# The first norm: block 0 of the context's norm ahead of the latents' statistics, modulation columns of blocks 4 to 7 loaded in pairs, matmuls at fixed places

## The chip, the cores and the metric

The kernel runs on one core of one Trainium2 chip, as one program. The metric is the device time of one execution in microseconds (us). Its engines are called by short names: PE is the matrix engine (PEld its weight loads), DVE the vector engine, ACT the scalar engine, POOL the GpSimd engine, and SP the engine that issues nearly all DMAs. Each engine takes its instructions strictly in the order in which the program lists them, and waits on semaphores for the others.

## The reference, cut to what matters

A backbone of two layers works on 256 latent tokens (x) and 256 context tokens (ctx) of width 1024. Only the head of the first layer is touched here: both streams are normed and modulated by columns that come from their conditions (c and c_ctx), and the result goes through the input projection.

```python
def rms_norm(x, g):
    xf = x.astype(F32)
    y = xf * lax.rsqrt(jnp.mean(xf * xf, axis=-1, keepdims=True) + EPS)
    return (y * g.astype(F32)).astype(x.dtype)

def adaln_norm(x, g, shift, scale):
    return rms_norm(x, g) * (1 + scale) + shift

mx = [m[:, None, :] for m in modulation(c, w_mod[l], b_mod[l])]   # silu(c) @ w + b, split in 6
mc = modulation(c_ctx, w_mod[l], b_mod[l])
h = adaln_norm(x, norm1_g[l], mx[0], mx[1])
hc = adaln_norm(xc, norm1_g[l], mc[0], mc[1])
... (hc @ w_in[l]) and (h @ w_in[l]), split into keys, values, queries, gates and so on
```

## The kernel before

Everything is kept transposed: the width of 1024 lies in 8 blocks of 128 partitions, the tokens lie along the free dimension. For accuracy each matmul operand is split into a high half (rounded) and a low half (what rounding took), and a product is three matmuls: high x high, high x low, low x high. PE is the engine that has nearly all the work.

first_norm() is the start of the program. It loads the tokens of both streams, forms their statistics (squares on ACT with a sum, then a reciprocal root by a dozen operations on 128x2 numbers on DVE, tile ss), and transposes the tokens on PE (xm). Stream 0 is the context, stream 1 the latents. Then it goes through the 8 blocks d of the width. For each block it
- multiplies the conditions by the block's modulation columns on PE ("rows", tile tp, line 592; the weights come by load_mod),
- copies the rows out (tile g) and turns them into columns by two small matmuls with the selector sel ("columns", line 607),
- forms modT (shift and scale), then na (scale times norm gain) on DVE,
- norms the block for each stream (norm_block): t = x * na * 1/rms on DVE, the high half h on ACT, and the low half h on DVE; for blocks 1, 3 and 5 (POOL_D) ACT adds the shift to t first and POOL forms the low half,
- multiplies the block's h with three chunks of the input projection (products, line 582), which accumulate over the blocks in six PSUM banks. One chunk and one block are 12 matmuls, 4 token tiles of 3.

The weights of the three chunks come in halves of four blocks (load_part): the load goes to raw or wq, ACT forms the high half (wh, br), and the low half (wl, br) is formed by POOL for chunks 0 and 2 and by DVE for chunk 1.

All DMAs of this stage are issued by SP in the order of the code, at most eight under way at a time. The order on the compute engines is set by a scheduler at build time, which follows the code and its own estimate of when operands are ready; tc.issue_after keeps an instruction behind another one. Behind the first norm the first gates follow (gates, line 345), whose weights load_w brings.

Of the kernel before, what the change touches and what calls it, by code (L numbers as in the profile page):

```python
# [10 lines left out]
F32 = mybir.dt.float32  # L11
# [5 lines left out]
ALU = mybir.AluOpType  # L17
AX = mybir.AxisListType

P = 128  # L20
D = 1024
T = 256
# [24 lines left out]
def kernel(ctx: ExitStack, tc: tile.TileContext, io, dbg=None, stop=None):  # L47
    nc = tc.nc
# [11 lines left out]
    def sb(tag, shape, dtype=F32):  # L60
        uid[0] += 1
        return pool.tile(shape, dtype, tag=tag, name=f"{tag}{uid[0]}", bufs=BUFS[tag])
# [87 lines left out]
    tp = ps("tp")  # L150
    nc.tensor.transpose(tp[:, 0:128], pk1, ident)
    nc.vector.tensor_copy(out=pkT[:, 0:128], in_=tp[:, 0:128])
    tp = ps("tp")
# [146 lines left out]
    COND = (1, 0)  # L300
# [205 lines left out]
    def first_norm():  # L506
# [6 lines left out]
        wmod, wt = {}, {}  # L513
        tags = ["r"] * 4 + ["wk"] * 2 + ["wa"] * 2 + ["a"] * 4 + ["z"] * 4

        def load_mod(d):
            wmod[d] = []
            for q in range(2):
                t_ = sb(tags[2 * d + q], [P, 4, 2, P])
                for m in range(2):  # L520
                    last_load[:] = [nc.sync.dma_start(out=t_[:, :, m, :], in_=src[:, 4 * q:4 * q + 4, m * D + d * P:m * D + (d + 1) * P])]
                wmod[d].append(t_)

        wide = []

# [11 lines left out]
            wt[ch, q] = (hi, lo)  # L537

        load_mod(0)
        load_tokens(1)  # L540
        sel = const.tile([P, 2], F32, name="sel")
        nc.vector.reduce_sum(out=sel, in_=_view(ident, 0, [(1, 2), (32, 4)]), axis=AX.X)
        rb = {}
        tps = ["mm"] * 3 + ["lv"] * 2 + ["mm"] * 3
        for st in range(2):
            ss = const.tile([P, 3, 2], F32, name=f"ss0{st}")
            for i in range(2):
                junk = sb("g2", [P, D], BF16)
                with tc.issue_after(sig.ins):
                    act(junk, tok_in[st, i], AF.Square, accum_out=ss[:, 0, i:i + 1])  # L550
            affine(ss[:, 0, :], ss[:, 0, :], 1.0 / D, EPS)
            rsqrt(ss[:, 1, :], ss[:, 0, :], ss[:, 2, :])
            for dd in range(4):
                tp = ps(tps.pop(0), (P, 2, T))
                for e in range(2):
                    for i in range(2):
                        c = (dd * 2 + e) * P
                        nc.tensor.transpose(tp[:, e, i * P:(i + 1) * P], tok_in[st, i][:, c:c + P], ident)
                if dd == 3 and st == 1:
                    nc.vector.tensor_copy(out=xT[st][:, 2 * dd:2 * dd + 2, :], in_=tp)  # L560
                else:
                    act(xT[st][:, 2 * dd:2 * dd + 2, :], tp, AF.Copy)
            rbc = ps("lv")
            for i in range(2):
                nc.tensor.matmul(rbc[:, i * P:(i + 1) * P], ss[:, 1, i:i + 1].to_broadcast([P, P]), ident, start=True, stop=True)
            rb[st] = sb("acc", [P, T])
            nc.vector.tensor_copy(out=rb[st], in_=rbc[:, 0:T])

        sums = [[ps("mm"), ps("mm")], [ps("mm"), ps("lv")], [ps("lv"), ps("lv")]]
        zero = sb("g2", [P, 512], BF16)  # L570
        nc.vector.memset(zero, 0.0)
        for b in sums[0] + sums[1] + sums[2]:
            nc.tensor.matmul(b, zero[:, 0:P], zero, start=True, stop=False)
        na = const.tile([P, 8, 2], F32, name="na0")

        def products(d, chunks, tiles=range(4)):
            for t in tiles:
# [6 lines left out]
                                             start=False, stop=(d == 7 and a_ == 1 and t % 2 == 1))  # L584
            return o

        order = {0: [(0, 0)], 1: [(1, 0)], 2: [(2, 0)], 3: [(0, 1), (1, 1)], 4: [(2, 1)]}
        for d in range(8):
            acc = ps("tp")
            for q in range(2):  # L590
                for j in range(4):
                    after = nc.tensor.matmul(acc[32 * j:32 * j + 32, 0:T], cT[:, 4 * q + j, :], wmod[d][q][:, j].rearrange("p m c -> p (m c)"),
                                     start=(q == 0), stop=(q == 1), tile_position=(0, 32 * j))
            for part in order.get(d, ()):
                load_part(*part)
            if d < 7:
                load_mod(d + 1)
            rows = sb("g2", [P, T])
            evac(rows, acc[:, 0:T])
            mt_ = ps("tp", (P, 2, 2))  # L600
            if d > 4:

                with tc.issue_after(after.ins):
                    after = products(d - 1, (0, 1, 2), (0, 1))
            with tc.issue_after(after.ins):
                for m in range(2):
                    after = nc.tensor.matmul(mt_[:, m, :], rows[:, m * P:(m + 1) * P], sel, start=True, stop=True)
            if d > 4:
                with tc.issue_after(after.ins):
                    products(d - 1, (0, 1, 2), (2, 3))  # L610
            tt(modT[:, 0, :, d:d + 9:8], mt_.rearrange("p m c -> p c m"),
               bmT[:, d:d + 9:8].unsqueeze(1).to_broadcast([P, 2, 2]), ALU.add)
            stt(na[:, d, :], modT[:, 0, :, 8 + d], 1.0, g1T[:, d:d + 1].to_broadcast([P, 2]), ALU.add, ALU.mult)
            for st in range(2):
                norm_block(0, st, 0, d, na[:, d, COND[st]:COND[st] + 1], rb[st], h)
            if d < 3:
                for ch in range(d + 1):
                    for dp in ([d] if ch < d else range(d + 1)):
                        products(dp, (ch,))
            elif d < 4:  # L620
                products(d, (0, 1, 2))
        for ch in range(3):
            products(7, (ch,))
        kv = sb("a", [P, 4, 256])
# [861 lines left out]
```

## Time and profile before

| | us |
|---|---|
| median of 3 runs | 1426.37 (1424.94 to 1430.34) |
| the profiled execution's own time | 1425.23 |
| its span, first to last instruction | 1423.1 |
| PE busy | 1399.8 (98% of the span) |
| DVE, ACT, POOL busy | 959.2, 675.4, 65.8 |
| granted TensorE clock, mean | 0.999 of full speed |

The profile's times are from one execution, counted from its first instruction. "Busy" for PE includes the tail of pipelined matmuls. A wait is put down to the semaphore that came last.

### The profile page before, as it was taken

The page shows a single profiled execution, that of the slowest core. Times are in us where ns is not written, and L with a number is a line of the kernel's source. Part 1 is how long each engine was busy: PE and PEld are TensorE (multiplying, and loading weights), DVE is VectorE, ACT ScalarE, POOL GpSimd, SP SyncE. Part 2 cuts the span into 40 slices and gives each one's busy share as a digit, 9 for nine tenths or more (in the row PEclk, how much of TensorE's full clock was granted, in tenths as well). Part 3 has the DMA queues.
Part 4 walks back from the last instruction along what each step waited for, and adds up shares of the span by engine and source line. Part 5 has one row for each costly group of instructions (what it writes and reads, how often), then busy time and mean ns, then how long its engine had stood idle before and what let it go on. Part 6 is the DMA issues. An engine that isn't in the chain of part 4 may idle for free.

```text
span 1423.1 us, 25125 instructions
## 1 busy us (share of the span) xinstructions
PE 1399.8 (98%) x10055; PEld 1224.8 (86%) x10056; DVE 959.2 (67%) x1824; ACT 675.4 (47%) x1253; POOL 65.8 (5%) x78
## 2 busy tenths in 40 slices
PE   7999999999999999999999999999999999999998
PEld 5887988899877789887777888998998999989987
DVE  5565757778884457996765445675779966765655
ACT  5445477464223335423314234465694645655543
POOL 2200001111000000000000000010002100000000
PEclk9999999999999999999999999999999999999999
DMA  9632212314864433576773332343234445665663
GB/s 313 224 101 78 60 60 72 90 32 122 282 225 159 133 127 96 183 229 205 256 236 120 106 100 89 90 124 90 71 104 135 121 134 178 180 190 164 192 193 119
DMA packets 165045, 205.75 MB, mean 145 GB/s; under 512 B 6784, under 2 KB 148640, under 8 KB 164416
## 3 DMA queue, kind: packets, MB, share of 16 engines
q1 hardware_dynamic: 164160, 201.44, 45.6%
q0 software_dynamic: 576, 2.62, 0.7%
q8 instruction: 79, 1.29, 0.4%
q14 instruction: 38, 0.31, 0.1%
q10 hardware_dynamic: 192, 0.08, 0.0%
HBM read 200.97 MB, written 3.15 MB: 143 GB/s over the span
## 4 chain that ended last, share of the span: by engine, by line
PE 92%; DVE 5%; DMA 1%; issue 1%; SPq 1%; ACT 1%; DVEq 0%; ACTq 0%
PE mm L345 17%; PE mm L347 17%; PE mm L346 17%; PE lv L1363 5%; PE mm L361 3%; PE mm L363 3%; PE mm L362 3%; PE tp L346 2%; PE tp L345 2%; PE tp L347 2%; PE lv L345 2%; PE lv L347 2%; PE lv L346 2%; PE tp L873 2%; PE mm L582 1%; PE tp L1363 1%
## 5 line engine op out<-in xcount | busy, mean ns | idle before, releaser
L86 DVE TENSOR_TENSOR wl<-raw,wh 128x1024 fp32r<-128x1024 f32 (+1 forms) x274 | 333.6, 1219 | 161.1 <-ACT wh L82 152.2
L82 ACT ACTIVATE wh<-raw 128x1024 fp32r<-128x1024 f32 (+1 forms) x278 | 289.8, 1046 | 301.3 <-PE mm L346 123.6
L345 PE MATMUL mm<-h,wh 128*128 128x512 f32 (+1 forms) x704 | 250.1, 355 | 0.8 <-DVE z L86 0.8
L347 PE MATMUL mm<-h,wl 128*128 128x512 f32 (+1 forms) x704 | 249.4, 355 | 0.7 <-DVE wl L86 0.6
L346 PE MATMUL mm<-h,wh 128*128 128x512 f32 (+1 forms) x704 | 248.9, 354 | 0.0
L345 PEld LDWEIGHTS mm<-h,wh 128*128 128x128 f32 x704 | 133.2, 189 | 26.4 <-ACT wh L82 2.5
L347 PEld LDWEIGHTS mm<-h,wl 128*128 128x128 f32 x704 | 133.1, 189 | 19.6 <-DVE wl L86 2.0
L346 PEld LDWEIGHTS mm<-h,wh 128*128 128x128 f32 x704 | 133.2, 189 | 17.0 <-issue 0.2
L345 PE MATMUL mm<-br,wh 128*128 128x258 f32 (+2 forms) x381 | 118.8, 312 | 0.0
L347 PE MATMUL mm<-br,wl 128*128 128x258 f32 (+2 forms) x381 | 118.1, 310 | 0.0
L346 PE MATMUL mm<-br,wh 128*128 128x258 f32 (+2 forms) x381 | 118.0, 310 | 0.0
L361 PE MATMUL mm<-wh,h 128*128 128x256 f32 x384 | 113.0, 294 | 0.6 <-DVE xm L86 0.6
L363 PE MATMUL mm<-wh,h 128*128 128x256 f32 x384 | 110.5, 288 | 0.0
L362 PE MATMUL mm<-wl,h 128*128 128x256 f32 x384 | 109.8, 286 | 0.0
L90 DVE SCALAR_TENSOR_TENSOR br<-wa,cT,br 128x1024 f32<-128x1024 f32 x56 | 70.5, 1279 | 24.6 <-DMA wa<-in_w_mod 24.5
L347 PEld LDWEIGHTS mm<-br,wl 128*128 128x128 f32 x381 | 72.1, 189 | 4.6 <-DVE g L86 0.8
L361 PEld LDWEIGHTS mm<-wh,h 128*128 128x128 f32 x384 | 74.0, 193 | 1.8 <-DVE xm L86 0.8
L345 PEld LDWEIGHTS mm<-br,wh 128*128 128x128 f32 x381 | 72.1, 189 | 4.0
L346 PEld LDWEIGHTS mm<-br,wh 128*128 128x128 f32 x381 | 72.2, 190 | 3.7
L362 PEld LDWEIGHTS mm<-wl,h 128*128 128x128 f32 x384 | 74.0, 193 | 0.5
L363 PEld LDWEIGHTS mm<-wh,h 128*128 128x128 f32 x384 | 74.0, 193 | 0.3 <-issue 0.2
L346 PE MATMUL mm<-r,wh 128*128 128x512 f32 (+1 forms) x208 | 70.6, 340 | 0.0
(390 smaller groups left out, 2899.1 us busy)
## 6 DMA issues: line engine op xcount, KB each, us to landing
raw<-in_w_ff SPq DMA_DIRECT2D x128, 512.0 KB, 3.7
raw<-in_w_in SPq DMA_DIRECT2D x106, 512.0 KB, 3.8
wa<-in_w_mod SPq DMA_DIRECT2D x64, 512.0 KB, 4.4
raw<-in_w_branch SPq DMA_DIRECT2D x24, 512.0 KB, 4.1
raw<-in_w_out SPq DMA_DIRECT2D x16, 512.0 KB, 3.7
wk<-in_w_mod SPq DMA_DIRECT2D x8, 512.0 KB, 6.1
wq<-in_w_mod SPq DMA_DIRECT2D x8, 512.0 KB, 6.2
r<-in_w_mod SPq DMA_DIRECT2D x8, 256.0 KB, 6.8
```

The lines of the kernel that those rows point to most:

```text
L82: return nc.scalar.activation(out=out, in_=in_, func=func, **kw)
L86: return nc.vector.tensor_tensor(out=out, in0=in0, in1=in1, op=op)
L90: return nc.vector.scalar_tensor_tensor(out=out, in0=in0, scalar=scalar, in1=in1, op0=op0, op1=op1)
L345: nc.tensor.matmul(o, w(0, kt, cs), act_h(kt)[:, c0:c1], start=(kt == 0), stop=False)
L346: nc.tensor.matmul(o, w(0, kt, cs), act_l(kt)[:, c0:c1], start=False, stop=False)
L347: nc.tensor.matmul(o, w(1, kt, cs), act_h(kt)[:, c0:c1], start=False, stop=(kt == nk - 1))
L361: nc.tensor.matmul(o, act_h(kt)[:, ts], w(0, kt, cs), start=(kt == 0), stop=False)
L362: nc.tensor.matmul(o, act_h(kt)[:, ts], w(1, kt, cs), start=False, stop=False)
L363: nc.tensor.matmul(o, act_l(kt)[:, ts], w(0, kt, cs), start=False, stop=(kt == 7))
L582: o = nc.tensor.matmul(sums[ch][t // 2][:, (t % 2) * T:(t % 2 + 1) * T], h[a_][d // 4][:, d % 4, ts], wt[ch, d // 4][w_][:, d % 4, :], sta ...
L873: nc.tensor.matmul(op[64 * hh:64 * hh + 64, i * P:(i + 1) * P], kv[:, vt, 128 + g * 64:192 + g * 64], pts[i][:, kt, hh, :], start=(kt == 0 ...
L1363: nc.tensor.matmul(acc[b], u(kt)[:, ts], w[part][:, cols[n]], start=(g + kt + m == 0), stop=(g == 3 and kt == 7 and m == 2))
```

## The change

Three things are changed in first_norm(). The first half of chunk 0's weights is loaded ahead of the latents' tokens, and block 0's rows, columns and context norm are written ahead of the latents' statistics. The modulation columns of blocks 4 and 5, and of 6 and 7, are loaded together: four tiles of two row blocks with 256 columns in place of two tiles of four row blocks with 128 columns for each block, so that a contiguous piece is 1 KB where it was 512 B. And from block 4 on the places of the rows and columns among the products are written out: block 3's products now stand behind block 3's norm in pieces by chunk, around the rows and columns of block 4, and block 5's around those of block 6.

```diff
         wmod, wt = {}, {}
         tags = ["r"] * 4 + ["wk"] * 2 + ["wa"] * 2 + ["a"] * 4 + ["z"] * 4
-        def load_mod(d):
-            wmod[d] = []
-            for q in range(2):
-                t_ = sb(tags[2 * d + q], [P, 4, 2, P])
+        def load_mod(d, n=1):
+            tiles = []
+            for q in range(2 * n):
+                t_ = sb(tags[2 * d + q], [P, 4 // n, 2, n * P])
                 for m in range(2):
-                    last_load[:] = [nc.sync.dma_start(out=t_[:, :, m, :], in_=src[:, 4 * q:4 * q + 4, m * D + d * P:m * D + (d + 1) * P])]
-                wmod[d].append(t_)
+                    c0 = m * D + d * P
+                    last_load[:] = [nc.sync.dma_start(out=t_[:, :, m, :], in_=src[:, 4 // n * q:4 // n * (q + 1), c0:c0 + n * P])]
+                tiles.append(t_)
+            for e in range(n):
+                wmod[d + e] = lambda kt, e=e: tiles[kt * n // 4][:, kt % (4 // n), :, e * P:(e + 1) * P]
         wide = []
...
             wt[ch, q] = (hi, lo)
         load_mod(0)
+        load_part(0, 0)
         load_tokens(1)
...
         tps = ["mm"] * 3 + ["lv"] * 2 + ["mm"] * 3
-        for st in range(2):
+        def statistics(st):
             ss = const.tile([P, 3, 2], F32, name=f"ss0{st}")
             for i in range(2):
                 junk = sb("g2", [P, D], BF16)
...
                 nc.tensor.matmul(rbc[:, i * P:(i + 1) * P], ss[:, 1, i:i + 1].to_broadcast([P, P]), ident, start=True, stop=True)
             rb[st] = sb("acc", [P, T])
             nc.vector.tensor_copy(out=rb[st], in_=rbc[:, 0:T])
+        na = const.tile([P, 8, 2], F32, name="na0")
+        def mod_rows(d):
+            acc = ps("tp")
+            for q in range(2):
+                for j in range(4):
+                    after = nc.tensor.matmul(acc[32 * j:32 * j + 32, 0:T].rearrange("p (m c) -> p m c", m=2), cT[:, 4 * q + j, :], wmod[d](4 * q + j),
+                                     start=(q == 0), stop=(q == 1), tile_position=(0, 32 * j))
+            return acc, after
+        def mod_columns(rows, mt_):
+            for m in range(2):
+                after = nc.tensor.matmul(mt_[:, m, :], rows[:, m * P:(m + 1) * P], sel, start=True, stop=True)
+            return after
+        def mod_block(d, mt_):
+            tt(modT[:, 0, :, d:d + 9:8], mt_.rearrange("p m c -> p c m"),
+               bmT[:, d:d + 9:8].unsqueeze(1).to_broadcast([P, 2, 2]), ALU.add)
+            stt(na[:, d, :], modT[:, 0, :, 8 + d], 1.0, g1T[:, d:d + 1].to_broadcast([P, 2]), ALU.add, ALU.mult)
+        statistics(0)
+        acc, _ = mod_rows(0)
+        load_mod(1)
+        rows = sb("g2", [P, T])
+        evac(rows, acc[:, 0:T])
+        mt_ = ps("tp", (P, 2, 2))
+        mod_columns(rows, mt_)
+        mod_block(0, mt_)
+        norm_block(0, 0, 0, 0, na[:, 0, COND[0]:COND[0] + 1], rb[0], h)
+        statistics(1)
...
             nc.tensor.matmul(b, zero[:, 0:P], zero, start=True, stop=False)
-        na = const.tile([P, 8, 2], F32, name="na0")
         def products(d, chunks, tiles=range(4)):
             for t in tiles:
...
                                              start=False, stop=(d == 7 and a_ == 1 and t % 2 == 1))
             return o
-        order = {0: [(0, 0)], 1: [(1, 0)], 2: [(2, 0)], 3: [(0, 1), (1, 1)], 4: [(2, 1)]}
+        order = {1: [(1, 0)], 2: [(2, 0)], 3: [(0, 1), (1, 1)], 4: [(2, 1)]}
+        def behind_of(after, *steps):
+            for step in steps:
+                with tc.issue_after(after.ins):
+                    after = step()
+            return after
         for d in range(8):
-            acc = ps("tp")
-            for q in range(2):
-                for j in range(4):
-                    after = nc.tensor.matmul(acc[32 * j:32 * j + 32, 0:T], cT[:, 4 * q + j, :], wmod[d][q][:, j].rearrange("p m c -> p (m c)"),
-                                     start=(q == 0), stop=(q == 1), tile_position=(0, 32 * j))
-            for part in order.get(d, ()):
-                load_part(*part)
-            if d < 7:
-                load_mod(d + 1)
-            rows = sb("g2", [P, T])
-            evac(rows, acc[:, 0:T])
-            mt_ = ps("tp", (P, 2, 2))
-            if d > 4:
-                with tc.issue_after(after.ins):
-                    after = products(d - 1, (0, 1, 2), (0, 1))
-            with tc.issue_after(after.ins):
-                for m in range(2):
-                    after = nc.tensor.matmul(mt_[:, m, :], rows[:, m * P:(m + 1) * P], sel, start=True, stop=True)
-            if d > 4:
-                with tc.issue_after(after.ins):
-                    products(d - 1, (0, 1, 2), (2, 3))
-            tt(modT[:, 0, :, d:d + 9:8], mt_.rearrange("p m c -> p c m"),
-               bmT[:, d:d + 9:8].unsqueeze(1).to_broadcast([P, 2, 2]), ALU.add)
-            stt(na[:, d, :], modT[:, 0, :, 8 + d], 1.0, g1T[:, d:d + 1].to_broadcast([P, 2]), ALU.add, ALU.mult)
-            for st in range(2):
+            if d > 0:
+                if d in (4, 6):
+                    after = products(d - 1, (0,))
+                    with tc.issue_after(after.ins):
+                        acc, after = mod_rows(d)
+                else:
+                    acc, after = mod_rows(d)
+                for part in order.get(d, ()):
+                    load_part(*part)
+                if d < 3:
+                    load_mod(d + 1)
+                elif d in (3, 5):
+                    load_mod(d + 1, 2)
+                rows = sb("g2", [P, T])
+                evac(rows, acc[:, 0:T])
+                mt_ = ps("tp", (P, 2, 2))
+                columns = lambda: mod_columns(rows, mt_)
+                if d < 4:
+                    columns()
+                elif d % 2:
+                    behind_of(after, lambda: products(d - 1, (0, 1, 2), (0, 1)), columns, lambda: products(d - 1, (0, 1, 2), (2, 3)))
+                else:
+                    behind_of(after, lambda: products(d - 1, (1,)), columns, lambda: products(d - 1, (2,)))
+                mod_block(d, mt_)
+            for st in ((0, 1) if d else (1,)):
                 norm_block(0, st, 0, d, na[:, d, COND[st]:COND[st] + 1], rb[st], h)
...
                         products(dp, (ch,))
-            elif d < 4:
-                products(d, (0, 1, 2))
         for ch in range(3):
             products(7, (ch,))
         kv = sb("a", [P, 4, 256])
```

What this does to the engines' order is shown at three places. The first is DVE, around block 0 of the context. g is the copy of block 0's rows, acc the copy of 1/rms of a stream, xm a stream's tokens, and ss_166 or ss_201 the latents' statistics. Before:

```order
L567 COPY acc_164<-lv_161 128x256
L571 MEMSET g_218 128x256
L122 TENSOR_SCALAR ss_166<-ss_166 128x2
L102 COPY g_250<-tp_227 128x256
L112 TENSOR_SCALAR ss_166<-ss_166 128x2
L560 COPY xm_98<-mm_201 128x512
L114 TENSOR_SCALAR ss_166<-ss_166 128x2
L86 TENSOR_TENSOR modT<-tp_252,pkT 128x2x2
L86 TENSOR_TENSOR ss_166<-ss_166 128x2
L90 SCALAR_TENSOR_TENSOR na_226<-modT,pkT 128x2
L90 SCALAR_TENSOR_TENSOR ss_166<-ss_166 128x2
L90 SCALAR_TENSOR_TENSOR t_257<-xm_97,na_226,acc_164 128x256
```

The same place of the change:

```order
L102 COPY g_190<-tp_175 128x256
L572 COPY acc_173<-lv_170 128x256
L86 TENSOR_TENSOR modT<-tp_192,pkT 128x2x2
L90 SCALAR_TENSOR_TENSOR na_128<-modT,pkT 128x2
L90 SCALAR_TENSOR_TENSOR t_197<-xm_97,na_128,acc_173 128x256
L608 MEMSET g_253 128x256
L90 SCALAR_TENSOR_TENSOR h_106<-t_197,modT,h_104 128x256
L122 TENSOR_SCALAR ss_201<-ss_201 128x2
L112 TENSOR_SCALAR ss_201<-ss_201 128x2
L565 COPY xm_98<-mm_236 128x512
L114 TENSOR_SCALAR ss_201<-ss_201 128x2
```

The context's block 0 moved as a whole ahead of the latents' statistics, where the two were interleaved. On ACT, likewise, the context's high half h of block 0 now stands between the squares of the latents' first and second token tile.

The second place is PE around block 3's columns (tp_484 before, tp_490 now); tp_535 and tp_517 are block 4's rows, wh_238 and wh_116 the high half of chunk 0, h_104 the high and h_106 the low half of the normed blocks 0 to 3. Before:

```order
L607 MATMUL tp_484<-sel,g_482 128x2 x2
L592 MATMUL tp_535<-a_476,cT 32x256 x4
L592 MATMUL tp_535<-a_479,cT 32x256 x4
L582 MATMUL mm_212<-wh_238,h_104 128x256
L582 MATMUL mm_212<-wl_239,h_104 128x256
L582 MATMUL mm_214<-wh_288,h_104 128x256
```

The same place of the change:

```order
L580 MATMUL tp_451<-wa_373,cT 32x256 x4
L586 MATMUL tp_490<-sel,g_488 128x2 x2
L618 MATMUL mm_247<-wh_116,h_104 128x256
L618 MATMUL mm_247<-wl_117,h_104 128x256
L618 MATMUL mm_248<-wh_116,h_104 128x256
L618 MATMUL mm_248<-wl_117,h_104 128x256
L618 MATMUL mm_247<-wh_116,h_106 128x256
```

Block 3's second half of rows (tp_451), which stood 54 products ahead of block 3's columns, now stands right ahead of them, and block 4's rows moved from behind the columns to behind twelve products of block 3.

The third place is ACT around block 5 (t_629 and t_634 before, t_635 and t_640 now, context and latents); wh_1731 and wh_1737 are splits of the first gate's weights, t_697 and t_701 are block 6. Before:

```order
L82 ACTIVATE h_105<-t_629,modT 128x256
L82 ACTIVATE h_105<-t_634,modT 128x256
L82 ACTIVATE t_629<-t_629,modT 128x256
L82 ACTIVATE t_634<-t_634,modT 128x256
L82 ACTIVATE wh_1731<-raw_1729 128x1024
L82 ACTIVATE h_105<-t_697,modT 128x256
```

The same place of the change:

```order
L82 ACTIVATE wh_1731<-raw_1729 128x1024
L82 ACTIVATE h_105<-t_635,modT 128x256
L82 ACTIVATE wh_1737<-raw_1735 128x1024
L82 ACTIVATE h_105<-t_640,modT 128x256
L82 ACTIVATE t_635<-t_635,modT 128x256
L82 ACTIVATE t_640<-t_640,modT 128x256
```

Both splits moved ahead: one before block 5's high halves, one between them.

## Rows read from the trace of the kernel before

**Rows 1.** Page, part 1: busy us, share of the span, instructions.
```profile
PE 1399.8 (98%) x10055; PEld 1224.8 (86%) x10056; DVE 959.2 (67%) x1824; ACT 675.4 (47%) x1253; POOL 65.8 (5%) x78
```
**Rows 2.** Windows: from:to, length, busy by engine (instructions), clock, DMA share, GB/s.
```profile
9.00:24.20 15.20, 13.03 (x93) 9.10 (x94) 10.27 (x38) 10.13 (x19) 2.50 (x2) 1.00 1.11 365
```
**Rows 3.** Waits of PE, whole run: us in total, times, longest.
```profile
PE lv L936 <- DVE wq L86: 3.0, 2, 1.9
...
PE mm L582 <- DVE h L90: 1.1, 1, 1.1
```
**Rows 4.** Timeline, first loads: start us, us, engine, what [idle before]; one landing.
```profile
13.31 1.06 ACT L82 ACTIVATE g<-z 128x1024 bf16<-128x1024 f32 x1 [0.84 <-DMA z<-in_x]
...
14.52 0.55 PE L558 MATMUL lv<-ident,z 128*128 128x128 f32 x3 [0.23 <-DMA z<-in_x]
...
9.47 0.43 SPq L528 DMA_DIRECT2D raw<-in_w_in  x1
...
DMA to landing us min/median/max: 6.4/6.4/6.4
```
**Rows 5.** Timeline from 14 to 22 us: ACT's second square, POOL, DVE, and PE's wait.
```profile
14.55 1.06 ACT L82 ACTIVATE g<-z 128x1024 bf16<-128x1024 f32 x1
...
15.73 0.17 DVE L122 TENSOR_SCALAR ss<-ss 128x2 f32<-128x2 f32 x1 [0.88 <-ACT g L82]
...
16.21 0.69 DVE L560 COPY xm<-mm 128x512 f32<-128x512 f32 x1
...
17.76 2.50 POOL L107 TENSOR_TENSOR wl<-raw,wh 128x512 fp32r<-128x512 f32 x2 [15.81 <-ACT wh L82]
...
17.91 1.13 DVE L86 TENSOR_TENSOR ss<-ss 128x2 f32<-128x2 f32 x1
19.08 1.40 DVE L90 SCALAR_TENSOR_TENSOR ss<-ss 128x2 f32<-128x2 f32 x2
...
20.59 0.48 DVE L90 SCALAR_TENSOR_TENSOR h<-t,modT,h 128x256 fp32r<-128x256 f32 x1
...
21.12 0.50 PE L582 MATMUL mm<-wh,h 128*128 128x256 f32 x2 [1.13 <-DVE h L90]
```
**Rows 6.** Timeline: the latents' first product, then block 3 on PE, DVE, POOL.
```profile
24.78 0.39 PE L582 MATMUL mm<-wh,h 128*128 128x256 f32 x1
...
35.38 4.12 PE L582 MATMUL lv<-br,h 128*128 128x256 f32 x33
39.34 0.51 PE L607 MATMUL tp<-sel,g 128*128 128x2 f32 x4
39.77 1.07 PE L592 MATMUL tp<-a,cT 128*32 128x256 f32 x16
41.42 0.39 PE L582 MATMUL mm<-wh,h 128*128 128x256 f32 x1 [0.58 <-ACT h L82]
...
40.34 0.88 DVE L90 SCALAR_TENSOR_TENSOR t<-xm,na,acc 128x256 f32<-128x256 f32 x2
...
34.96 2.56 POOL L107 TENSOR_TENSOR br<-wq,br 128x512 fp32r<-128x512 f32 x2
42.25 0.73 POOL L423 TENSOR_TENSOR h<-t,h 128x256 fp32r<-128x256 f32 x1 [4.74 <-ACT t L82]
```
**Rows 7.** A load, its landing; queue rows (packets, MB, share) of 34.2:41, 70:75; a split.
```profile
33.08 0.98 SPq L528 DMA_DIRECT2D raw<-in_w_in  x1
...
DMA to landing us min/median/max: 5.9/5.9/5.9
...
q1 hardware_dynamic: 4041, 2.27, 109.7%
...
q1 hardware_dynamic: 478, 0.49, 33.0%
...
52.77 1.06 ACT L82 ACTIVATE wh<-raw 128x1024 fp32r<-128x1024 f32 x1
```
**Rows 8.** Timeline of PE: the first matmul behind the first norm.
```profile
68.33 0.40 PE L345 MATMUL mm<-h,wh 128*128 128x512 f32 x1
```

## The prediction

> **What bounds the kernel now.** I read the page's head first: TensorE (PE) is busy 1399.8 of 1423.1 us [rows 1], so whatever changes the time must change PE's idle time. The windows then say where idle time is: the stretch from 9.0 to 24.2 us is the one part of the first norm where PE is not full (13.03 of 15.20 busy), at full granted clock [rows 2]. The list of PE's waits confirms it: the one wait in that stretch that the edit aims at is 1.1 us for VectorE's (DVE) low half h of block 0, and the longest entry that lies outside the first norm is 3.0 us [rows 3]. So the edit can win two or three microseconds of 1423 at most, and each microsecond that PE newly waits in the first norm is lost: nothing behind it is long enough to take it back. Finer reading goes by the timeline, an engine at a time.
>
> **What the present order pays for.** The first token tile of the latents lands at 13.3 us, the second at 14.5, and the load queued behind them, issued at 9.47 with 6.4 to landing, at 15.9 [rows 4]. DVE starts the latents' statistics at 15.73, and between them stands the context's block 0. From 17.76 to 20.26 GpSimd (POOL) forms two low halves of a weight tile, and in just that stretch two DVE operations on 128x2 numbers take 1.13 and 1.40 us (for two) where their like take 0.17; so the low half h starts at 20.59 and PE waits 1.13 us [rows 5]. That reading matters below. A DVE operation with two operands in SBUF that meets a POOL operation stands until POOL's instruction ends; one of them passes between two POOL instructions. The Trainium skill, "SBUF — State Buffer", section "SBUF: two separate sides", says the same: the pair of ports that the two engines share is an exclusive lock, held for the whole instruction, against a DVE operation with two SBUF inputs. By that rule the sum is the one below; without it the sum would be some 2 us less. The trace agrees with it here.
>
> **The change part by part, term a: up to block 3's columns.** The first weight part now takes the first token tile's place in the queue and lands at 13.3; the tokens land at 14.5 and 15.9, 1.2 and 1.4 us later [rows 4]. ScalarE (ACT) splits the part by 14.0 and POOL forms its low halves from 14.0 to 16.5 (two of 1.25 [rows 5]). That is exactly where the context's block 0 now runs on DVE: its na waits until 15.3, its t until 16.5, so t ends at 17.0 and ACT's high half at 17.6. The square of the second token tile stands behind that high half on ACT: it starts at 17.6 instead of 15.9, and ends with its sum at 18.9 (1.06 + 0.19 + gaps). Twelve small DVE operations at 0.2 each and the 0.69 copy put the latents' statistics at 22.0; then in DVE's new order a copy 0.42, a weight half 0.68, the copy of the norm 0.42, a half 0.68, modT 0.2 and t 0.48 lead to 25.0, and ACT and PE follow at 25.6 with the latents' first product. Now that product starts at 24.78; PE will by then have done one half of modulation rows more (0.57), so the stage stands 0.25 us later, although PE no longer waits 1.13 us for block 0. From 25.6 on PE has 96 products at 0.12 (33 in 4.12 less the tail [rows 6]), two halves of rows at 0.57, block 2's columns 0.45 and about 0.4 of waits: 39.1. There the new order puts block 3's columns right behind the rows that they need: 0.6 for the copy in between, 0.45 for themselves, 40.15, against 39.77 now [rows 6]. Term a: +0.4. Without the shared ports the high half would come 1.35 us sooner: -0.95. If the tokens' 1.4 us come through whole: +1.4.
>
> **Term b: block 3.** Now the 1.0 us of block 4's rows follows those columns, so of the chain columns, modT, na, t, h (39.34 to 41.42) PE waits only 0.58; and the first products after it need high halves alone, so the low half that POOL ends at 42.98 is waited for by no one [rows 6]. In the changed order block 3's twelve products of the first chunk come before block 4's rows, four of them need the high halves and the fifth a low half. What POOL does then is the second half of the third chunk's weights (now at 34.96 [rows 6], long done when block 3 comes). Its load has gone behind eight loads of modulation columns; it takes the place of the load issued at 33.08, which with 5.9 to landing is 39.0 [rows 7]. The eight loads have 1 KB pieces now. From two windows a 512 B piece took 1.097 x 16 x 6.8 / 4041 = 29.5 ns of an engine, a 1 KB piece 0.33 x 16 x 5 / 478 = 55 [rows 7]: 6% less, 0.4 us of their 6.8. I take 38.55. ACT's first split half then ends at 39.2, and POOL is busy from 39.2 to 41.75, over block 3's na (40.4) and t. So t starts at 41.8 instead of 40.65, the high half ends at 42.8, PE starts at 42.85. Four products take it to 43.35; ACT's two identities and POOL's 0.73 bring the low half at 44.5, the second at 45.25. PE ends the twelve at 45.75 and block 4's rows at 46.85. From 40.15 that is 6.7 us, against 3.1 now (39.77, 1.0 of rows, 0.58, 1.44 for twelve products, switches): +3.6. If POOL is done before t, t is bound by the columns alone and this is +1.6; with the load at 39.0 it is +4.2.
>
> **Term c: block 5.** It has a POOL low half too. Block 5's columns begin at 53.5 (46.85 and 12 products, columns, 12 products, rows, 18 products: 6.6 us). Its t ends at 54.9. In the new order ACT has a split of 1.06 us [rows 7] for the next stage between the two high halves, where it now stands behind all of block 5. High halves: 55.5 and 57.05; low halves by POOL about 58.5 and 59.25. PE has 18 products to 56.15 as cover, then twelve of block 5: it waits for the second high half 0.7, for the low ones 1.1 and 0.4, and is done at 59.7 where 57.6 would be free of waits: +2.0 (1.0 without the split, 2.6 if POOL loses to DVE's own halves at that point). For block 4, 6 and 7 the cover is 2.4 us against a chain of 2.1, with low halves on DVE: nothing.
>
> The loads of pairs free the queue 0.8 us sooner for the next stage, whose PE is full: nothing. **Sum:** 0.4 + 3.6 + 2.0 = +6.0 us; between the bounds +1.7 and +8.2. On the profiled execution's own 1425.23 this is 1431.2; the median of the runs lies 1.1 above it, so 1432.
>
> **The rivals.** *Late weights, slower beyond doubt.* If the third chunk's second half lands late, everything in term b behind POOL moves one for one. It decides from 39.65 us (1.1 after my 38.55): +7.1 and more, say +8, 1434.4. For it: it now queues behind eight loads; against: 5.9 us to landing in the same place [rows 7], and 1 KB pieces cost no more.
>
> *The ports hold less than I read.* If t passes between POOL's instructions in both places, a becomes -0.95 and b 2.9: +4, 1430.4. For it: na does pass; against: 1.13 and 1.40 [rows 5].
>
> *The change does what it says.* Block 0 takes 1.13 us from PE's idle time, block 3 costs no more than its 0.58, block 5 nothing: -1.1, 1425.3. For it: PE's one long wait there is real [rows 3, 5]. Against: PE takes its instructions in order, and the new order has two rows back to back that need a DVE copy between them.
>
> **How the numbers follow.** Chances: the forecast 0.55, late weights 0.22, ports 0.15, gain 0.08. A range of 1426 to 1435 leaves out the gain and the tail of the late weights. A measurement of this kernel can tell about 0.5% (7.1 us) from no change. Slower than that: most of the late weights and the forecast's upper edge, 0.24. Faster than that would need more idle time than the first norm has behind its first loads, 0.02. Within: 0.74.
>
> **What would show it.** Right: DVE's t of block 0 ends near 17 us beside POOL; PE's first product of the latents near 25.6; between block 3's columns and block 4's rows PE idles 3 to 4 us, with POOL forming a weight's low half just before; ACT has a 1.06 us split between block 5's high halves; the first matmul of the next stage starts near 74 us instead of 68.33 [rows 8], and from there on both programs run side by side. Wrong: a first norm that ends at 68 or earlier; DVE undisturbed beside POOL; or a difference that arises behind 75 us, where I put none.

## The result, and the profile after

The changed kernel takes 1433.99 us (median of 6 runs, 1433.38 to 1435.55) beside 1425.65 of the kernel before: a ratio of 1.0057, 95% interval 1.0045 to 1.0069, which is 8.3 us more. The prediction of 1432 was 2 us short, inside its range of 1426 to 1435. The median lies 1.2 us beyond the 0.5% that a measurement can tell from no change, and the interval lies on both sides of that bound. The profiled execution took 1435.55 us with a span of 1433.4.

The page's first part, for [rows 1]:

```profile
PE 1405.1 (98%) x10055; PEld 1228.5 (86%) x10056; DVE 960.2 (67%) x1824; ACT 675.1 (47%) x1253; POOL 66.0 (5%) x78
```

PE's work has not changed, but 5.3 us more of the span counts as busy. Of these 3.6 lie ahead of the first matmul behind the first norm (busy 62.05 us up to there, 58.41 before). The windows (columns as in [rows 2]) show the stretch in which PE was slow:

```profile
9.00:24.20 15.20, 13.36 (x101) 9.43 (x101) 10.35 (x40) 9.91 (x19) 2.50 (x2) 1.00 1.11 366
...
39.30:50.00 10.70, 7.92 (x49) 6.05 (x50) 2.61 (x6) 1.70 (x4) 3.50 (x5) 0.68 1.05 388
...
42.00:44.00 2.00, 1.60 (x6) 1.31 (x6) 0.00 (x0) 1.16 (x3) 1.16 (x2) 0.50 1.07 431
44.00:46.00 2.00, 2.00 (x12) 1.60 (x15) 0.00 (x0) 0.00 (x0) 0.75 (x2) 0.50 1.03 430
46.00:48.00 2.00, 2.00 (x18) 0.90 (x11) 0.37 (x1) 0.00 (x0) 0.00 (x0) 0.50 0.95 306
```

From 9 to 24.2 us PE does 0.33 us more than before; that edit gives little. From 39.3 to 50 us it is busy only 7.92 of 10.70, with a granted clock of 0.68; between 42 and 48 us the clock is 0.50, the lower of its two levels, 1.2 GHz. Before, the clock over the whole stretch up to 68.33 us is 1.00. The waits of PE, for [rows 3]:

```profile
PE mm L618 <- ACT h L82: 2.8, 2, 2.4
PE mm L345 <- ACT a L82: 2.1, 1, 2.1
...
PE mm L610 <- DVE xm L565: 1.4, 1, 1.4
PE mm L618 <- POOL h L423: 1.3, 2, 0.9
...
PE tp L586 <- DVE g L102: 0.5, 1, 0.5
```

The wait for block 0's low half (1.1) is gone; in its place stands one of 1.4 for VectorE's copy of the latents' last token blocks. New are 2.4 us for a high half, 1.3 for two low halves of POOL, and 2.1 in a later stage. The timeline, an engine at a time, answers to [rows 4 to 8]; products now stand at L618, rows at L580, columns at L586:

```profile
13.77 2.50 POOL L107 TENSOR_TENSOR wl<-raw,wh 128x512 fp32r<-128x512 f32 x2 [11.83 <-ACT wh L82]
...
15.26 1.30 DVE L90 SCALAR_TENSOR_TENSOR t<-xm,na,acc 128x256 f32<-128x256 f32 x1
...
24.94 0.39 PE L618 MATMUL mm<-wh,h 128*128 128x256 f32 x1
...
31.54 0.37 SPq L532 DMA_DIRECT2D wq<-in_w_in  x1
...
37.70 1.15 ACT L82 ACTIVATE br<-wq 128x512 fp32r<-128x512 f32 x2 [4.65 <-DMA wq<-in_w_in]
...
38.40 2.48 POOL L107 TENSOR_TENSOR br<-wq,br 128x512 fp32r<-128x512 f32 x2 [3.83 <-ACT br L82]
...
39.86 1.04 DVE L90 SCALAR_TENSOR_TENSOR na<-modT,pkT 128x2 f32<-128x2 f32 x1
40.94 0.88 DVE L90 SCALAR_TENSOR_TENSOR t<-xm,na,acc 128x256 f32<-128x256 f32 x2
...
39.02 0.61 PE L586 MATMUL tp<-sel,g 128*128 128x2 f32 x4 [0.55 <-DVE g L102]
42.02 0.58 PE L618 MATMUL mm<-wh,h 128*128 128x256 f32 x1 [2.39 <-ACT h L82]
...
43.62 0.80 PE L618 MATMUL mm<-wh,h 128*128 128x256 f32 x2 [0.38 <-POOL h L423]
...
45.63 1.94 PE L580 MATMUL tp<-a,cT 128*32 128x256 f32 x16
47.49 0.58 PE L618 MATMUL mm<-wh,h 128*128 128x256 f32 x1
...
54.58 0.51 PE L586 MATMUL tp<-sel,g 128*128 128x2 f32 x4
...
58.02 0.38 PE L618 MATMUL mm<-wh,h 128*128 128x256 f32 x1 [0.44 <-ACT h L82]
...
59.46 0.50 PE L618 MATMUL mm<-wh,h 128*128 128x256 f32 x2 [0.94 <-POOL h L423]
...
60.82 1.07 PE L580 MATMUL tp<-z,cT 128*32 128x256 f32 x16
...
75.49 0.40 PE L345 MATMUL mm<-h,wh 128*128 128x512 f32 x1
```

The reader is to see the chain at 38 us: weights land, ACT splits, POOL takes 2.48 us, and in that time DVE's na, an operation on 128x2 numbers, takes 1.04 us, where it took 0.16 before:

```profile
40.08 0.16 DVE L90 SCALAR_TENSOR_TENSOR na<-modT,pkT 128x2 f32<-128x2 f32 x1
```

Then come t, the high half and the first product. PE has stood for 2.39 us by then and goes on at half clock (block 4's rows take 1.94 us instead of 1.07). The first matmul behind the first norm, the gate, comes at 75.49 instead of 68.33 [rows 8]: +7.16 of the +10.32 us between the two profiled executions.

### The profile page after: what moved, and what is told of

Read it like the earlier page. It is cut to its first block, busy times and chain, and to the rows that moved or that the text cites. A ratio compares the mean times of both kernels' runs of the same rounds, so it can differ in the third digit from the quotient of the medians.

```text
span 1433.4 us, 25126 instructions
## 1 busy us (share of the span) xinstructions
PE 1405.1 (98%) x10055; PEld 1228.5 (86%) x10056; DVE 960.2 (67%) x1824; ACT 675.1 (47%) x1253; POOL 66.0 (5%) x78
## 3 DMA queue, kind: packets, MB, share of 16 engines
HBM read 200.97 MB, written 3.15 MB: 142 GB/s over the span
## 4 chain that ended last, share of the span: by engine, by line
PE 87%; DVE 6%; DMA 5%; issue 1%; ACT 1%; POOL 0%; SPq 0%; DVEq 0%; ACTq 0%
PE mm L346 16%; PE mm L345 16%; PE mm L347 16%; PE lv L1405 5%; DMA wa<-in_w_mod 4%; PE mm L361 3%; PE mm L363 3%; PE mm L362 3%; PE tp L346 2%; PE tp L345 2%; PE tp L347 2%; PE tp L915 2%; PE lv L346 1%; PE lv L345 1%; PE tp L1405 1%
```

## The experiments

Each median is of 5 to 12 runs, and each ratio is to the kernel before as it ran beside that kernel (medians of before from 1425.65 to 1426.16). Two places in PE's row order them: the start of block 3's columns (39.34 before, 39.02 changed) and the gate. The stretch between, 28.99 us before and 36.47 changed, leaves out how early a run's tokens came.

| kernel | columns | gate | between | median us | ratio to before (95%) |
|---|---|---|---|---|---|
| before | 39.34 | 68.33 | 28.99 | 1425.65 | |
| changed | 39.02 | 75.49 | 36.47 | 1433.99 | 1.0057 (1.0045 to 1.0069) |
| pairs alone | 40.81 | 70.34 | 29.53 | 1427.08 | 1.0008 (1.0000 to 1.0017) |
| block 0 alone | 39.40 | 68.42 | 29.02 | 1426.36 | 1.0002 (0.9993 to 1.0011) |
| old places | 39.49 | 69.77 | 30.28 | 1428.24 | 1.0016 (1.0005 to 1.0028) |
| old places, early load | 39.32 | 68.36 | 29.04 | 1425.14 | 0.9994 (0.9986 to 1.0003) |
| early load | 38.94 | 74.82 | 35.88 | 1433.26 | 1.0055 (1.0043 to 1.0067) |
| rows of block 4 first | 39.17 | 74.68 | 35.51 | 1434.50 | 1.0057 (1.0043 to 1.0070) |
| three undoings | 39.57 | 69.87 | 30.30 | 1428.10 | 1.0014 (1.0005 to 1.0023) |
| 16 extra matmuls | 39.37 | 75.75 | 36.38 | 1433.78 | 1.0050 (1.0037 to 1.0062) |
| low halves 3, 5 on DVE | 38.51 | 71.89 | 33.38 | 1429.87 | 1.0028 (1.0018 to 1.0038) |
| the same, extra matmuls | 39.01 | 69.88 | 30.87 | 1427.92 | 1.0013 (1.0004 to 1.0022) |
| low half 5 on DVE | 39.28 | 75.33 | 36.05 | 1432.98 | 1.0046 (1.0033 to 1.0059) |
| token copy first | 38.93 | 67.96 | 29.03 | 1425.36 | 0.9998 (0.9989 to 1.0007) |

The medians follow the gate within some 2 us, so the gate is the finer reading.

**The parts of the change.** First each alone, then the changed kernel with its places undone:

```diff
...
-            if d < 7:
-                load_mod(d + 1)
+            if d < 3:
+                load_mod(d + 1)
+            elif d in (3, 5):
+                load_mod(d + 1, 2)
...
```

> The kernel before with one part of the change: the modulation columns of blocks 4 to 7 come in pairs, the order of the work is the old one. Theory (the places cost, the loads only shift POOL): the third chunk's second half now lands near 38 us, POOL forms its low half over block 3's na and t as in the changed kernel, t is about 1 us later, PE's wait for block 3's high half grows from 0.58 to about 1.5 us; the first gate matmul stands at 69.3 us (before 68.33, changed kernel 75.49), time about 1426.5. Rival (the late half is the cause of most of the loss): the gate at 72 us or later, 1429 or more. Rival (larger pieces free the queue and help): the gate at 68 us or earlier.

Between columns and gate it is +0.54, but the gate stands 1.0 us later than expected, and the theory's cause did not occur. PE stood 1.54 us for block 0's low half (1.13 before), its clock was 0.50 from 22 to 24 us, and block 3's columns came 1.5 us later than before. By then POOL was done with the late half, and na took 0.16 us:

```profile
37.38 2.55 POOL L107 TENSOR_TENSOR br<-wq,br 128x512 fp32r<-128x512 f32 x2 [1.05 <-ACT br L82]
...
41.55 0.16 DVE L90 SCALAR_TENSOR_TENSOR na<-modT,pkT 128x2 f32<-128x2 f32 x1
```

PE's wait at block 3 is 0.78 us for DVE's copy of block 4's rows. So the time agrees with the first theory, but this run does not show POOL's half over block 3; the old places below do.

> The kernel before with another part alone: block 0 of the context, its norm and the first weight part ahead of the latents' statistics; single loads and the old places from block 1 on. Theory: block 3's columns stand within 0.3 us of where they stood in the kernel before, since the 1.13 us that PE no longer waits there come back as later tokens and a wait for the copy of the second token tile; the first gate matmul at 68.0 to 68.5 us, time 1425.5 +-0.7. Rival (the reorder does what it is for): the gate at 67.2, 1.1 us earlier, time 1424.5. Rival (the reorder costs by itself): the gate at 69 or later.

```diff
-        for st in range(2):
...
+        statistics(0)
+        acc, _ = mod_rows(0)
...
+        norm_block(0, 0, 0, 0, na[:, 0, COND[0]:COND[0] + 1], rb[0], h)
+        statistics(1)
```

The gate stands at 68.42, as the theory had it, and the time cannot be told from before. What PE no longer waits for the low half it waits, 1.7 us here, for the token copy.

> The changed kernel with the matmuls of blocks 3 to 7 in the old places (block 3's products behind block 4's rows, the products of blocks 4 to 6 two halves around the columns); block 0 ahead and the pair loads stay. Theory (fixed places take the cover away): terms b and c go but for what POOL's later low half costs: the first gate matmul at 69 us, time about 1426.5, no stretch at half clock near 42 us. Rival (late weights are the cause): the gate at 73 us or later, 1431 or more, with the same stretch at half clock.

```diff
-                if d in (4, 6):
-                    after = products(d - 1, (0,))
...
+                acc, after = mod_rows(d)
...
+            elif d < 4:
+                products(d, (0, 1, 2))
```

Of the 7.5 us between columns and gate 6.2 are gone, and no stretch of the first norm is at half clock: the fixed places are the cause of these 6.2. The gate is still 0.8 us later than expected. What is left shows in the timeline:

```profile
40.33 1.21 DVE L90 SCALAR_TENSOR_TENSOR na<-modT,pkT 128x2 f32<-128x2 f32 x1
...
42.84 0.61 PE L586 MATMUL tp<-sel,g 128*128 128x2 f32 x4 [1.75 <-DVE g L102]
```

na stands beside POOL, and DVE's copy of block 4's rows stands behind it. If that is all, an earlier load takes it away:

> The changed kernel with the matmuls of blocks 3 to 7 in the old places and the third chunk's second half asked for ahead of the pair loads: what stays of the change is block 0 ahead and the pairs themselves. Theory (what the pairs cost in the old places, 30.28 us from columns to gate against 29.02 with single loads, is only POOL's low half over block 3's na): na takes 0.16 us instead of 1.21, PE's 1.75 us wait for the copy of block 4's rows goes, columns to gate 29.0 to 29.2, time within 0.7 us of before. Rival (the pairs delay something else): 30 us or more.

```diff
-        order = {1: [(1, 0)], 2: [(2, 0)], 3: [(0, 1), (1, 1)], 4: [(2, 1)]}
+        order = {1: [(1, 0)], 2: [(2, 0)], 3: [(0, 1), (1, 1), (2, 1)]}
```

```profile
40.17 0.16 DVE L90 SCALAR_TENSOR_TENSOR na<-modT,pkT 128x2 f32<-128x2 f32 x1
```

The stretch is 29.04, as expected, and the whole loss of 7.48 is placed: 6.19 by the places and 1.24 by the late half, undone in this order. In the other order the half gives 0.59 (the next kernel) and the places 6.84, so the two shares are not independent.

**Inside term b.** The same early load in the changed kernel, and block 4's rows put back ahead of block 3's products:

> The changed kernel with one load moved: the third chunk's second half is asked for ahead of the modulation columns of blocks 4 and 5 instead of behind them. Theory: POOL is done with it before block 3's columns, na takes 0.2 instead of 1.04 us, PE's first product of block 3 starts near 41.0 instead of 42.02 us and still has no cover; the first gate matmul moves from 75.49 to 74.5 if the clock still falls behind the stall, to about 72.6 if the shorter stall keeps the clock; time 1433.0 or 1431. Rival (POOL plays no part, the chain of columns alone sets it): the gate stays within 0.3 us of 75.49. Rival (the late half is all of it): the gate at 70 or earlier.

```profile
39.78 0.16 DVE L90 SCALAR_TENSOR_TENSOR na<-modT,pkT 128x2 f32<-128x2 f32 x1
...
41.06 0.58 PE L618 MATMUL mm<-wh,h 128*128 128x256 f32 x1 [1.51 <-ACT h L82]
```

> The changed kernel with one place undone: block 4's rows stand ahead of block 3's products of the first chunk instead of behind them. Theory (these rows were the cover of block 3's chain): they run while DVE and ACT make the high half, PE waits 1.3 us instead of 2.39, and the gate moves by the 1.0 us of the rows, to 74.4; to about 72.6 if the shorter stand also keeps the clock. Rival (the order of the two pieces is indifferent, the low halves set the pace): the gate within 0.3 us of 75.49.

```diff
-                if d in (4, 6):
+                if d == 4:
+                    acc, after = mod_rows(d)
+                    with tc.issue_after(after.ins):
+                        after = products(d - 1, (0,))
+                elif d == 6:
```

The early load brings the first product to 41.06, as said, and the gate only 0.67 us forward: the clock still falls, and block 5 loses 0.4 us more. With the rows first the clock falls too (0.56 from 44 to 46 us), and PE waits 1.77 instead of 1.3 us, because the half lands 0.8 us later in this run and POOL stands over t; the gate moves 0.81 of the 1.0 us, the time not at all. Neither suffices alone; together with the third undoing they do:

> The changed kernel with three undoings together: block 4's rows ahead of block 3's products, the third chunk's second half asked for early, and the low halves of blocks 3 and 5 on VectorE. Theory (cover, POOL over na, and POOL's low halves are the whole of terms b and c, and the clock follows the stand): PE waits about 0.5 us for block 3's high half, the clock stays at 1.00, and the gate stands at 69.3 us, 0.9 behind the kernel that has block 0 ahead alone (68.42); time about 1427. Rival (fixed places cost something else as well): the gate at 71 or later.

The clock stays at 1.00 and PE waits 0.51 us for block 3. The stretch is 30.30, 1.28 over block 0 alone where I had allowed 0.9; 0.95 of it is a wait for a high half of block 6 that I had not foreseen.

**The clock.** Sixteen matmuls that nobody needs, where PE stands:

> The changed kernel with 16 extra matmuls of 128x256 (block 0's first product again, into a bank that nobody reads) put on PE between block 3's columns and block 3's products, where PE idles 2.39 us; at 0.12 us each they end before block 3's high half does, if the clock is full. Theory (the half clock from 41 to 48 us comes from PE standing still and costs about 1.9 us of term b): the granted clock stays at 1.00 from 39 to 50 us, products and rows go at 0.12 us and 1.0 us again, and the first gate matmul stands at 73.6 us instead of 75.49; time 1432.0. Rival (the clock falls for another reason): the clock is at half again, the fillers take 0.21 us each and push the gate to 76 or later. A gate at 75.5 with full clock would say that the half clock cost nothing.

```diff
...
+                        spare = ps("tp")
+                        for _ in range(16):
+                            with tc.issue_after(cols3.ins):
+                                cols3 = nc.tensor.matmul(spare[:, 0:T], h[0][0][:, 0, 0:P], wt[0, 0][0][:, 0, :], start=True, stop=True)
...
```

```profile
39.30:50.00 10.70, 9.71 (x84) 8.11 (x88) 3.86 (x11) 2.54 (x6) 3.63 (x5) 1.00 1.05 394
```

```profile
39.83 2.16 PE L640 MATMUL tp<-wh,h 128*128 128x256 f32 x16
42.21 0.38 PE L618 MATMUL mm<-wh,h 128*128 128x256 f32 x1 [0.22 <-ACT h L82]
...
45.17 1.07 PE L580 MATMUL tp<-a,cT 128*32 128x256 f32 x16
...
58.20 0.51 PE L618 MATMUL mm<-wh,h 128*128 128x256 f32 x2 [2.04 <-POOL h L423]
...
56.79 2.05 POOL L423 TENSOR_TENSOR h<-t,h 128x256 fp32r<-128x256 f32 x2 [11.89 <-ACT t L82]
```

Half the theory is shown: full clock, and from block 3's first product to the end of block 4's rows 3.96 us instead of 5.47. The gate did not move forward (75.75), which the expectation had named as a sign that the half clock cost nothing. It cannot be read so, because block 5 changed as well: ACT's split now stands behind both high halves, PE waited 2.04 us for POOL's low halves, and the clock fell behind that stand. The pair of kernels below, without POOL there, shows the price alone:

> The changed kernel with the low halves of blocks 3 and 5 in the first norm on VectorE instead of GpSimd. Theory: PE's waits for POOL's low halves (1.3 us in two) go, a VectorE low half takes 0.45 us behind the high one; the first product of block 3 still starts near 42.0 and the clock still falls; the gate at 74.5 us, time 1433. Rival (POOL's low halves were the point of term c): the gate at 73.5 or earlier. Rival (VectorE is too full here): 75.5 or later.

```diff
-        if d in POOL_D:
+        if d in POOL_D and not (l == 0 and which == 0 and d > 1):
```

> The changed kernel with the low halves of blocks 3 and 5 on VectorE and the 16 extra matmuls on PE between block 3's columns and its products. Without the extra matmuls PE stood 3.26 us there and its clock was at half until 45 us: columns to gate 33.38. Theory (standing still lowers the clock and the lowered clock costs 1.2 us there): the granted clock stays at 1.00 from 39 to 62 us, columns to gate 32.0 to 32.3. Rival (the clock falls anyway or costs nothing): 33.3 or more.

The kernel with the low halves on DVE, then the one with extra matmuls as well:

```profile
42.37 0.58 PE L618 MATMUL mm<-wh,h 128*128 128x256 f32 x1 [3.26 <-ACT h L82]
...
46.35 0.39 PE L618 MATMUL mm<-wh,h 128*128 128x256 f32 x1
...
53.09 0.51 PE L586 MATMUL tp<-sel,g 128*128 128x2 f32 x4
...
57.22 1.07 PE L580 MATMUL tp<-z,cT 128*32 128x256 f32 x16
```

```profile
41.54 0.39 PE L618 MATMUL mm<-wh,h 128*128 128x256 f32 x1
...
44.33 0.39 PE L618 MATMUL mm<-wh,h 128*128 128x256 f32 x1
```

From the first product to the end of block 4's rows it is 3.98 us where the clock fell, 2.79 with extra matmuls: 1.19, as expected. The stretch itself, 30.87, is 1.1 us shorter than the theory's 32.0. The other 1.3 us between the two kernels come from a half that landed 1.1 us sooner, so that POOL stood over less of the chain.

**Term c.** The low halves on DVE won 3.1 us between columns and gate, not the 1.0 I had said, so the rival was right about the gate: from block 5's columns (53.09) to block 6's rows 4.13 us, without a wait, where the changed kernel has 6.24. So I tried block 5 alone:

> The changed kernel with the low half of block 5 alone on VectorE. Measured from the start of block 3's columns to the first gate matmul, which takes out how early the tokens came: before 28.99 us, changed kernel 36.47, with the low halves of blocks 3 and 5 on VectorE 33.38. Theory (term c is GpSimd's low half of block 5 and nothing else, block 3 is as it was): 2.0 us less, 34.4 to 34.5, the stretch at half clock behind block 3 stays, no wait of PE for a low half near 58 us. Rival (ScalarE's weight split between the two high halves is half of term c): 35.4, with a wait for the second high half left.

```profile
56.92 1.05 ACT L82 ACTIVATE wh<-raw 128x1024 fp32r<-128x1024 f32 x1
...
58.32 1.22 DVE L86 TENSOR_TENSOR wl<-raw,wh 128x1024 fp32r<-128x1024 f32 x1
...
58.42 0.39 PE L618 MATMUL mm<-wh,h 128*128 128x256 f32 x1 [0.44 <-ACT h L82]
...
59.99 0.50 PE L618 MATMUL mm<-wh,h 128*128 128x256 f32 x2 [0.59 <-DVE h L90]
```

A miss: 5.68, only 0.56 less. ACT's split still stands between the two high halves, and now a weight half of DVE stands between the low ones. In the kernel with 3 and 5 on DVE the order made at build time had put both splits and both weight halves behind block 5. So its 4.13 us are not the price of POOL's low halves alone.

**A better one?**

> A try at a version better than both: the kernel with block 0 ahead alone (single loads, old places), and VectorE's copy of the latents' last two token blocks put ahead of the small operations of their statistics. With block 0 ahead alone PE waits 1.7 us for that copy before the zero matmuls and the first products. If that wait is on the path, it shrinks to about 0.9 us and the gate comes 0.5 to 0.8 us sooner than 68.42, at 67.6 to 67.9; time 1425.5, which a measurement here can't tell from before. If the latents' statistics, now 0.2 to 0.7 us later, set the path instead, the gate stays at 68.4 or goes later.

```profile
18.30 0.38 PE L614 MATMUL mm<-g 128*128 128x512 bf16 x1 [0.44 <-DVE xm L563]
```

The copy wait falls from 1.7 to 0.44 us, but a new one of 0.55 for VectorE's copy of the rows takes back a good part: the gate is 0.46 us sooner than with block 0 alone, 0.37 sooner than before. In time neither this one nor the old places with the early load can be told from before.

## Why the prediction was right, and where its terms were off

**What agreed and what was luck.** From the start of block 3's columns to the gate the change added 7.48 us, and with the columns 0.32 sooner the gate came 7.16 later; the prediction had 6.0. Term a came out -0.3, term b 5.0 and term c 2.1; the other 0.3 is the lower clock behind block 4's rows. Of the signs named, the split between block 5's high halves and POOL ahead of the stand came as said. PE's idle time at block 3 was 2.8 us (2.39 and 0.38), not 3 to 4. That the time lies within 2 us of 1432 is in part luck: term a was too high by 0.7, term b too low by 1.4.

**Term a, +0.4: measured -0.3** (columns at 39.02 against 39.34). The mechanism was right: POOL's weight halves lie over block 0's t, which took 1.30 us. But the weights landed sooner, and POOL's halves ended at 16.27 instead of 16.5; t ended at 16.56 instead of 17.0, and the latents' first product came at 24.94 instead of 25.6. The prediction gave the right reason for no gain, later tokens, only in part: the saved 1.13 us are also the new wait for the token copy, which it did not name.

**Term b, +3.6: mis-sized, and with a cost left out.** The place, POOL over na, and the wait for a low half came as said; the first product started 3.00 us behind the start of the columns (forecast 3.15). But POOL did not stand over t, which took 0.88 us for two as before: the load was asked for at 31.54 us, not 33.08, and landed at 37.7, not 38.55, so POOL was done at 40.88, just ahead of t. I had counted a 1 KB piece at 55 ns, from a short window, against two pieces of 512 B at 29.5, from a row that holds pieces of both sizes [rows 7]. This kernel's queue row from 32.2 to 38.2 us, in which the pairs run,

```profile
q1 hardware_dynamic: 2365, 2.30, 108.5%
```

gives 1.085 x 16 x 6.0 / 2.30 = 45 ns of an engine per KB; the row of before gives 1.097 x 16 x 6.8 / 2.27 = 53. That is 14% less, not 6%. The Trainium skill, "DMA: Bandwidth & Descriptors", section "Specifications", gives 512 B as the smallest transfer at line rate; here pieces twice as long still moved more per us, and the measurement decides. What the prediction left out is the lower clock. It counted block 4's rows at 1.0 us and products at 0.12 behind a stand of 2.4 us; they took 1.94 and 0.21. From the first product to the end of block 4's rows it had 4.0 us; at full clock, with the extra matmuls, they are 3.96, and in the changed kernel 5.47. So the 1.5 us are the clock (1.2 in the second pair of kernels).

How term b comes to 5.0: from the columns' start to the end of block 4's rows the changed kernel takes 8.47 us. In the kernel with both low halves on DVE and extra matmuls PE goes from there to the gate without a wait, in 25.55 us; that leaves 3.44 of the 28.99 us before for the same pieces.

**Term c, +2.0: measured 2.1** (6.24 against 4.13 us free of waits). The parts were not additive, as the prediction had them ("1.0 without the split"): with the split behind both high halves (the early load, the extra matmuls) block 5 took 6.63 and 6.84, since POOL's two low halves then met DVE's weight halves and took 2.05; with POOL taken out and the split left it took 5.68. It is 4.13 only in kernels where POOL, the split and DVE's weight halves are all out of the way. The prediction's 2.6 "if POOL loses to DVE's own halves" is that case (2.5 and 2.7).

**Behind 75 us, nothing forecast.** A difference that arises there was named as a sign of being wrong. The two profiled executions do drift 3.1 us further apart there, at four places: +0.6 by 270 us (attention, whose instructions the build orders a little differently), +1.8 near 700 us (PE waits 2.1 us for ACT's a, 0.5 before), -0.5 near 740, +1.2 near 1106 us, where the changed kernel ran longer at half clock. The first is steady: the seven kernels here with that other order of attention lose 0.4 to 0.6 us there, those with the old order at most 0.2. The rest is not: in the twelve kernels above, with that part of the program all but unchanged, time less gate is 1355.3 to 1358.6 us in the profiled executions; before has 1356.9 and this execution, the slowest of its six, 1360.1. So most of the 3.1 is this execution's, and the medians' 8.3 us are the first norm's 7.2, some 0.5 in attention, and a rest that these runs don't settle.

**The rivals.** Late weights: the half landed 0.85 us sooner than forecast, far from the 39.65 that this rival needed, so the case did not occur, though the time is close to its 1434.4. Ports hold less: block 0's t took 1.30 us beside POOL's halves, where an undisturbed one takes 0.48; na took 1.04 us and ended at 40.90, with POOL's second half (40.88), and takes 0.16 without POOL (early load). The Trainium skill, "SBUF — State Buffer", section "SBUF: two separate sides", has a VectorE operation with two SBUF inputs stand until a GpSimd instruction that began first ends; the runs agree. Does what it says: refuted by the result, and its gain from block 0 by that part alone, whose gate is at 68.42.

## What to carry to other kernels

Before a piece of work is moved on an engine that takes its instructions in order, ask what it covered. Here the moved places cost 6.2 us, though the rows of block 4 are 1.0 us of work; those rows alone put back won 0.8 us, and only with the other two undoings came most of it back. Where TensorE will stand for microseconds, allow for the price of its lower clock behind the stand beside the wait itself (1.2 to 1.5 us here, though not every stand was followed by it). A transfer that nobody waits for still matters by when it triggers another engine's work: one load moved ahead of eight won 1.2 us with the old places, 0.6 with the new.

## What the chip showed that was not expected

PE's granted clock fell to 0.50 behind stands of 1.51 to 3.26 us (1.51 with the early load, 1.54 with the pairs alone, 2.39 in the changed kernel), and matmuls that do nothing useful in that gap kept it at 1.00. A stand of 1.75 us (old places, between two groups of rows) left it at 1.00. In block 5 the same stand of 2.04 us left it at 1.00 with the early load, but not with the 16 extra matmuls ahead of block 3 (0.50 from 60 to 62 us). The windows of these two, in that order:

```profile
50.00:62.00 12.00, 9.96 (x94) 8.17 (x94) 5.42 (x11) 4.32 (x8) 2.05 (x2) 1.00 0.45 140
...
50.00:62.00 12.00, 9.96 (x85) 7.61 (x78) 4.81 (x10) 3.79 (x7) 2.05 (x2) 0.89 0.47 143
```

So the length of a stand alone does not tell; what else does stays open. The Trainium skill, "TensorE: Matmul & The Clock Gate", section "Part 1: The HAM clock gate", has the clock go by how busy TensorE was of late; the extra matmuls in the gap agree with that, and the two stands of 2.04 us neither show nor refute it.
